# The MLP's second product of a diffusion trunk: all token tiles by one tile of weights in five banks, its weight sums on VectorE, and a fixed matmul order where the MLP begins

## The chip, the cores and the metric

The kernel runs on one core of a Trainium2 chip. The metric is the device time of one execution in microseconds (us), from three runs of each kernel. Five engines work side by side: TensorE (PE in the rows; its weight loads are PEld), VectorE (DVE), ScalarE (ACT), GpSimd (POOL) and SyncE (SP), which issues the transfers from and to HBM. Matmuls write into banks of PSUM; the other operands lie in SBUF.

## The reference, cut to what matters

One layer of a transformer over 128 context tokens and 512 latent tokens with shared weights, in float32. The change is in the last third, the MLP and the step into it:

```python
# _layer, D_MODEL = 1024, D_FF = 4096
y = _merge((o_a, o_b, o_c, o_d), u['gates'], P)          # ends with @ P['w_out']
x = x + g1 * _rmsnorm(y, P['norm_mix_post'])
h = _rmsnorm(x, P['norm_mlp_pre']) * (1 + sc2) + sh2
y = jnp.square(jax.nn.relu(h @ P['w_mlp_in'])) @ P['w_mlp_out']
x = x + g2 * _rmsnorm(y, P['norm_mlp_post'])
```

## The kernel before

The 640 tokens are five tiles of 128 (`NT = 5`; tiles 0 to 3 latent, tile 4 context). A float32 product is made from high and low parts: each operand is split into `hi` (rounded) and `lo` (the rest), and three matmuls, hi by hi, hi by lo and lo by hi, replace one. A weight tile is loaded raw (`wr`, 128x1024), copied to `wh` (by ACT, or by POOL in `copy_r`, line 139) and its rest `wl` is taken by DVE (`rest`, line 142). The tags `wr`, `wh` and `wl` have three buffers each in SBUF.

**The end of the mixing block.** For each token tile the second column half of `w_out` is multiplied (`tok_block`, 24 matmuls, lines 381 to 383), normed (`finish_half`, `finish`), normed again for the MLP (line 1293), and `to_h2` turns it: eight transposes on PE (`tp`, line 1243), eight scaled copies on ACT (`h2f`, line 1246), the high part on POOL, the low part on DVE. The result `h2T` is kept in two halves of 320 tokens (`HALF`), so that tile 2 lies in both halves and tile 4 is the last 128 columns of the second.

**The MLP** goes over eight quarters `qd` (`NQ = 8`) of 512 hidden features. Quarter 0 is made plainly: four blocks `m` by two halves of tokens, 24 matmuls of 128x320 each (`products`, lines 1319 to 1321). Each other quarter is two calls of `pair`: seven products of 12 matmuls (128x320), a scheme that saves one product in eight by sums of weights (`weight_sums`, lines 1347 to 1352) and sums of tokens (`token_sums`, `tsum`); its results are put together by adds (line 1371), squared after the relu (line 1310) and split again into `hid`. A product goes into one of five PSUM banks of the tag `pr`.

**The second product** of quarter `qd` is `out_of(qd)`: for each column half `j` two weight tiles (four blocks of 128 hidden features), and for each token tile 12 matmuls of 128x512 into one of two banks of the tag `mm`; then `done` adds the bank to the running sum `y2` on DVE (line 1402; a copy on ACT for quarter 0, line 1400). Only in the last quarter the half j = 0 goes otherwise: five banks, the first two blocks of weights over all five token tiles, then the other two. In the last quarter `done` also scales by the norm's gains on POOL (line 1260), norms (lines 1265 and 1269) and writes out.

The program's order is `pair(1,0)`, `out_of(0)`, `pair(1,1)`, `pair(2,0)`, `out_of(1)`, and so on, with `out_of(qd)` ahead of the second pair of the quarter after; a scheduler then orders the instructions of each engine by simulated time, except in stretches under `in_order`, which chains all instructions of an engine in the order in which they are written. "A period" below is what recurs: one `out_of` (120 matmuls of 128x512) and two pairs (168 of 128x320).

Of the kernel before, what the change touches and what calls it, by code (L numbers as in the profile page):

```python
# [17 lines left out]
D = 1024  # L18
# [46 lines left out]
def trunk(ctx, tc, I, O):  # L65
# [1214 lines left out]
    for tt in range(NT):  # L1280
        finish_half(banks[tt], x1(tt), tt, 0, G1, ssqs[:, 0, tt], V)
    w = [(w_hi[:, k], w_lo[:, k]) for k in range(4)] + wgroup(wo, 512, 512, k0=4, nk=4)
    for tt in range(NT):
        ps = tok_block(w, 512, yX, tt)
        finish_half(ps, x1(tt), tt, 1, G1, ssqs[:, 0, tt], V)
        x = mxa.tile([128, D], F32, tag="x", name="x", bufs=3)
# [50 lines left out]
    def weight_sums(c0):  # L1337

        r1, r2 = (wload(w1, 0, c0 + 128 * m, 128, 8) for m in range(2))
        sa = wp.tile([128, 1024], F32, tag="wr", name="ws")  # L1340
        p, q = slice(0, 512), slice(512, 1024)

        def split(x, nk):
            hi, lo = wsplit(x, 128, nk)
            return [[(hi[:, k], lo[:, k]) for k in range(i, i + 4)] for i in range(0, nk, 4)]
        a11, a12 = split(r1, 8)
        V.tensor_tensor(out=sa[:, q], in0=r2[:, p], in1=r2[:, q], op=ALU.add)  # L1347
        V.tensor_tensor(out=sa[:, p], in0=sa[:, q], in1=r1[:, p], op=ALU.subtract)
        g2, g1 = split(sa, 8)
        G.tensor_tensor(out=r2[:, p], in0=r1[:, p], in1=r2[:, p], op=ALU.subtract)  # L1350
        g3, a22 = split(r2, 8)
        G.tensor_tensor(out=r1[:, q], in0=r1[:, q], in1=sa[:, p], op=ALU.subtract)
        g4, = split(r1[:, q], 4)
        return a11, a12, a22, g1, g2, g3, g4

    def pair(c0, X, hid):
# [9 lines left out]
        def part(name):  # L1366
            return mxb.tile([128, HALF], F32, tag=name, name=name, bufs=1)

        def add(eng, p, q, out=None):
            out = relu2_tile() if out is None else out  # L1370
            eng.tensor_tensor(out=out, in0=p, in1=q, op=ALU.add)
# [40 lines left out]
    def out_of(qd):  # L1412

        for j in range(2):
            w = wgroup(w2, 512 * j, 512, k0=4 * qd, nk=4)
            if qd == NQ - 1 and j == 0:

                banks = [psl.tile([128, 512], F32, tag="pr", name="last", bufs=5) for _ in range(NT)]
                for k in (0, 2):
                    for tt in range(NT):  # L1420
                        tok_block(w[k:k + 2], 512, hid[qd][k:k + 2], tt, banks[tt], start=(k == 0), stop=(k == 2))
                        if k:
                            done(qd, tt, j, banks[tt])
                continue
            for tt in range(NT):
# [3 lines left out]
    hid[0] = [x for _ in range(2) for x in blocks_of(big(F32R, 2, 2, T, name="hid"))]
    for ms in ((0, 1, 2), (3,)):  # L1430
        ws = {m: wgroup(w1, 128 * m, 128) for m in ms}
        for th in range(2):
            for m in ms:
                ps, sq = mm_tile()[:, 0:HALF], relu2_tile()
                products(ps, ws[m], by_k(h2[0][th]) + by_k(h2[1][th]))
                S.activation(out=sq, in_=ps, func=AF.Relu)
                to_hid(sq, hid[0][m], HALF * th)
# [49 lines left out]
```

## Time and profile before

| | before |
|---|---|
| median of 3 runs | 1496.71 us |
| lowest and highest | 1494.04 and 1497.32 us |
| the profiled execution, its own time | 1497.44 us |
| its span, first to last instruction | 1495.7 us |
| mean granted TensorE clock | 0.989 |
| busy: PE, DVE, ACT, POOL | 94%, 61%, 35%, 32% of the span |

The span is 1.7 us shorter than the profiled execution's own time, and that execution is 0.7 us longer than the median. Times in the rows are counted from the span's start. The MLP begins at about 1019 us, where the transposes of tile 2 follow the last matmul of `w_out`, and its last matmul starts at 1484.57. A busy PE counts the modelled length of each matmul, which is longer than the distance from one start to the next; distances between starts tell its pace.

### The profile page before, as it was taken

The page shows a single profiled execution, that of the slowest core. Times are in us where ns is not written, and L with a number is a line of the kernel's source. Part 1 is how long each engine was busy: PE and PEld are TensorE (multiplying, and loading weights), DVE is VectorE, ACT ScalarE, POOL GpSimd, SP SyncE. Part 2 cuts the span into 40 slices and gives each one's busy share as a digit, 9 for nine tenths or more (in the row PEclk, how much of TensorE's full clock was granted, in tenths as well). Part 3 has the DMA queues.
Part 4 walks back from the last instruction along what each step waited for, and adds up shares of the span by engine and source line. Part 5 has one row for each costly group of instructions (what it writes and reads, how often), then busy time and mean ns, then how long its engine had stood idle before and what let it go on. Part 6 is the DMA issues. An engine that isn't in the chain of part 4 may idle for free.

```text
span 1495.7 us, 26614 instructions
## 1 busy us (share of the span) xinstructions
PE 1411.4 (94%) x10801; PEld 1279.3 (86%) x10801; DVE 909.8 (61%) x1587; ACT 519.7 (35%) x1189; POOL 481.6 (32%) x486
## 2 busy tenths in 40 slices
PE   6999999999999999999998998999999999899997
PEld 5898999999898998999996677988887888888885
DVE  4347757476643787433725566748755757857756
ACT  4334333333443235442125565226331221211212
POOL 2015326243322435222314334125322322223224
PEclk9999999999999999999999999999999999999998
DMA  9421222131112131113224601232213512312221
GB/s 331 127 85 58 72 58 59 44 75 43 45 46 57 43 75 37 41 35 78 78 66 162 205 15 43 99 88 68 85 57 113 155 43 85 99 43 85 86 82 72
DMA packets 138227, 121.17 MB, mean 81 GB/s; under 512 B 22297, under 2 KB 119413, under 8 KB 138105
## 3 DMA queue, kind: packets, MB, share of 16 engines
q1 hardware_dynamic: 138104, 119.47, 26.9%
q8 instruction: 85, 1.39, 0.4%
q14 instruction: 38, 0.30, 0.1%
HBM read 115.96 MB, written 3.49 MB: 80 GB/s over the span
## 4 chain that ended last, share of the span: by engine, by line
PE 68%; DVE 15%; POOL 5%; issue 5%; ACT 4%; DMA 3%; POOLq 0%; DVEq 0%; ACTq 0%
PE mm L365 8%; PE mm L366 8%; PE mm L367 8%; PE mm L381 5%; PE mm L382 5%; PE mm L383 5%; DVE wl L142 4%; PE tp L860 3%; PE pv L1013 3%; PE sc L383 3%; PE sc L381 2%; PE sc L382 2%; PE sc L953 2%; DVE relu L1310 2%; PE sc L954 2%
## 5 line engine op out<-in xcount | busy, mean ns | idle before, releaser
L142 DVE TENSOR_TENSOR wl<-wr,wh 128x1024 fp32r<-128x1024 f32 (+3 forms) x174 | 214.1, 1234 | 133.7 <-POOL wh L139 94.9
L139 POOL TENSOR_SCALAR wh<-wr 128x1024 fp32r<-128x1024 f32 (+2 forms) x108 | 123.5, 1147 | 341.5 <-PE mm L366 113.3
L365 PE MATMUL mm<-hTh,wh 128*128 128x320 f32 x704 | 220.4, 313 | 2.0 <-DVE qA L520 0.9
L367 PE MATMUL mm<-hTh,wl 128*128 128x320 f32 x704 | 219.1, 311 | 0.0
L366 PE MATMUL mm<-hTl,wh 128*128 128x320 f32 x704 | 218.1, 310 | 0.0
L813 POOL TENSOR_SCALAR P<-P,rden 128x640 f32<-128x640 f32 (+3 forms) x120 | 84.9, 717 | 183.5 <-DVE rden L825 87.3
L365 PEld LDWEIGHTS mm<-hTh,wh 128*128 128x128 f32 x704 | 132.2, 188 | 3.9 <-DVE qA L520 1.0
L367 PEld LDWEIGHTS mm<-hTh,wl 128*128 128x128 f32 x704 | 132.2, 188 | 0.9 <-issue 0.7
L366 PEld LDWEIGHTS mm<-hTl,wh 128*128 128x128 f32 x704 | 132.2, 188 | 0.5 <-issue 0.3
L382 PE MATMUL mm<-wl,hid 128*128 128x512 f32 x300 | 118.6, 395 | 4.8 <-DVE wl L142 4.8
L381 PE MATMUL mm<-wh,hid 128*128 128x512 f32 x300 | 117.2, 396 | 4.3 <-DVE y L1402 3.1
L383 PE MATMUL mm<-wh,hid 128*128 128x512 f32 x300 | 117.6, 392 | 0.0
L329 ACT ACTIVATE wh<-wr 128x1024 fp32r<-128x1024 f32 (+1 forms) x66 | 63.6, 965 | 90.9 <-PE mm L383 55.4
L1402 DVE TENSOR_TENSOR y<-mm,y 128x512 f32<-128x512 f32 x65 | 44.5, 687 | 68.0 <-PE mm L383 67.9
L381 PE MATMUL sc<-wh,hTh 128*128 128x256 f32 (+2 forms) x224 | 71.8, 321 | 5.4 <-DVE tx L939 2.4
L1321 PE MATMUL pr<-tsum,wl 128*128 128x320 f32 x224 | 69.0, 314 | 7.5 <-DVE wl L142 7.5
L860 PE MATMUL tp<-ident,P 128*128 128x128 f32 x456 | 72.5, 280 | 3.0 <-DVE modcol L242 1.1
L598 POOL TENSOR_TENSOR hk<-hk,hf 128x640 f32<-128x640 f32 x28 | 56.2, 2028 | 55.9 <-DVE hf L599 25.1
L1350 POOL TENSOR_TENSOR wr<-wr 128x512 f32<-128x512 f32 x14 | 31.2, 2228 | 132.3 <-DVE ws L1347 132.3
L381 PEld LDWEIGHTS mm<-wh,hid 128*128 128x128 f32 x300 | 56.5, 189 | 19.5 <-DVE y L1402 5.7
L382 PEld LDWEIGHTS mm<-wl,hid 128*128 128x128 f32 x300 | 56.7, 189 | 17.9 <-DVE wl L142 6.5
L383 PE MATMUL sc<-wh,hTl 128*128 128x256 f32 (+2 forms) x224 | 71.1, 317 | 0.2
(392 smaller groups left out, 3778.7 us busy)
## 6 DMA issues: line engine op xcount, KB each, us to landing
wr<-in_w_in SPq DMA_DIRECT2D x56, 512.0 KB, 3.8
wada<-in_w_ada SPq DMA_DIRECT2D x48, 512.0 KB, 4.9
wr<-in_w_mlp_in SPq DMA_DIRECT2D x32, 512.0 KB, 4.2
wr<-in_w_mlp_out SPq DMA_DIRECT2D x32, 512.0 KB, 3.7
wr<-in_w_in SPq DMA_DIRECT2D x64, 64.0 KB, 2.2
wr<-in_w_branch SPq DMA_DIRECT2D x8, 512.0 KB, 3.9
wr<-in_w_branch SPq DMA_DIRECT2D x16, 256.0 KB, 4.2
wr<-in_w_out SPq DMA_DIRECT2D x8, 512.0 KB, 3.6
```

Of the source, the lines that this page charges most:

```text
L139: G.tensor_scalar(out=out, in0=src, scalar1=1.0, scalar2=1.0, op0=ALU.mult, op1=ALU.mult)
L142: V.tensor_tensor(out=out, in0=src, in1=f(hi), op=ALU.subtract)
L329: S.activation(out=hi[:, 0:m], in_=raw[:, 0:m], func=AF.Copy)
L365: PE.matmul(out=ps[:, 0:tn], lhsT=wh, rhs=a, start=(k == 0), stop=False)
L366: PE.matmul(out=ps[:, 0:tn], lhsT=wh, rhs=b, start=False, stop=False)
L367: PE.matmul(out=ps[:, 0:tn], lhsT=wl, rhs=a, start=False, stop=(k == nk - 1))
L381: PE.matmul(out=ps[:, 0:n], lhsT=a, rhs=w[k][0], start=(start and k == 0), stop=False)
L382: PE.matmul(out=ps[:, 0:n], lhsT=a, rhs=w[k][1], start=False, stop=False)
L383: PE.matmul(out=ps[:, 0:n], lhsT=b, rhs=w[k][0], start=False, stop=(stop and k == nk - 1))
L813: G.tensor_scalar(out=Pt[:, i, 0:W], in0=Pt[:, i, 0:W], scalar1=rden[:, i:i + 1], scalar2=1.0, op0=ALU.mult, op1=ALU.mult)
L860: PE.transpose(out=tp[:, kk, i], in_=Pt[:, i, 128 * (kt + kk):128 * (kt + kk) + 128], identity=ident)
L1321: PE.matmul(out=ps, lhsT=w[k][1], rhs=x[k][0], start=False, stop=(stop and k == len(w) - 1))
```

## The change

Three things are changed. (1) `out_of` takes, for every quarter and both halves j, five `pr` banks; the first two blocks of weights (one `wr` tile) go over all five token tiles, then the other two, and `done` of a token tile comes after its second part. (2) Two of the weight sums of a pair and two of its adds are on DVE instead of POOL. (3) At the MLP's seam the PE order is written out under `in_order(PE)`: the norm's transposes of a token tile come two tiles later, three blocks of the first half of tokens come between those of tiles 2, 3 and 4, and block 0 of the second half is split into its first 192 and its last 128 columns, so that it has 48 matmuls instead of 24. The fourth block of quarter 0 follows after.

```diff
-    for tt in range(NT):
+    xs = {}
+    def second_half(tt):
         ps = tok_block(w, 512, yX, tt)
...
-        for kh in range(2):
-            to_h2(x, tt, kh)
+    def second_norm(tt):
+        for kh in range(2):
+            to_h2(xs[tt], tt, kh)
...
+    def block(w, m, th, parts=((0, HALF),)):
+        ps, sq = mm_tile()[:, 0:HALF], relu2_tile()
+        for a, b in parts:
+            products(ps[:, a:b], w, [(x[:, a:b], y[:, a:b]) for x, y in by_k(h2[0][th]) + by_k(h2[1][th])])
+        S.activation(out=sq, in_=ps, func=AF.Relu)
+        to_hid(sq, hid[0][m], HALF * th)
...
+    with in_order(PE):
+        for tt in range(NT):
+            second_half(tt)
+            if tt >= 2:
+                second_norm(tt - 2)
...
+        for m in range(3):
+            ws[m] = wgroup(w1, 128 * m, 128)
+            block(ws[m], m, 0)
+            if m:
+                second_norm(m + 2)
+        mn.close()
+        block(ws[0], 0, 1, ((0, 192), (192, HALF)))
+        for m in range(1, 3):
+            block(ws[m], m, 1)
...
         g2, g1 = split(sa, 8)
-        G.tensor_tensor(out=r2[:, p], in0=r1[:, p], in1=r2[:, p], op=ALU.subtract)
+        V.tensor_tensor(out=r2[:, p], in0=r1[:, p], in1=r2[:, p], op=ALU.subtract)
         g3, a22 = split(r2, 8)
-        G.tensor_tensor(out=r1[:, q], in0=r1[:, q], in1=sa[:, p], op=ALU.subtract)
+        V.tensor_tensor(out=r1[:, q], in0=r1[:, q], in1=sa[:, p], op=ALU.subtract)
...
-        u4 = add(G, u2, p5, part("u4"))
+        u4 = add(u2, p5, part("u4"))
...
-        to_hid(add(G, u3, p5), hid[1], HALF)
+        to_hid(add(u3, p5), hid[1], HALF)
...
             w = wgroup(w2, 512 * j, 512, k0=4 * qd, nk=4)
-            if qd == NQ - 1 and j == 0:
-                banks = [psl.tile([128, 512], F32, tag="pr", name="last", bufs=5) for _ in range(NT)]
...
-            for tt in range(NT):
-                done(qd, tt, j, tok_block(w, 512, hid[qd], tt))
+            banks = [psl.tile([128, 512], F32, tag="pr", name="out", bufs=5) for _ in range(NT)]
+            for k in (0, 2):
+                for tt in range(NT):
+                    tok_block(w[k:k + 2], 512, hid[qd][k:k + 2], tt, banks[tt], start=(k == 0), stop=(k == 2))
+                    if k:
+                        done(qd, tt, j, banks[tt])
```

**On PE, at the end of a period.** `mm` and `out` are banks of the second product (the number tells banks apart), `hid` its tokens, `pr` banks of the next pair's products. Before, from the second token tile of j = 1 on:

```order
L381 MATMUL mm_13827<-wh_13823,hid_13439 128x512
L382 MATMUL mm_13827<-wl_13824,hid_13439 128x512
L383 MATMUL mm_13827<-wh_13823,hid_13439 128x512
L1319 MATMUL pr_13925<-h2T_10873,wh_13903 128x320
L1320 MATMUL pr_13925<-h2T_10873,wh_13903 128x320
L1319 MATMUL pr_13939<-h2T_10875,wh_13903 128x320
L1320 MATMUL pr_13939<-h2T_10875,wh_13903 128x320
L381 MATMUL mm_13841<-wh_13817,hid_13119 128x512
L382 MATMUL mm_13841<-wl_13818,hid_13119 128x512
L383 MATMUL mm_13841<-wh_13817,hid_13119 128x512
```

The same place of the change, from the last part of the first pass into the second, and then the end of the half:

```order
L381 MATMUL out_13855<-wh_13841,hid_13143 128x512
L382 MATMUL out_13855<-wl_13842,hid_13143 128x512
L383 MATMUL out_13855<-wh_13841,hid_13143 128x512
L381 MATMUL out_13851<-wh_13847,hid_13463 128x512
L382 MATMUL out_13851<-wl_13848,hid_13463 128x512
L383 MATMUL out_13851<-wh_13847,hid_13463 128x512
```
```order
L382 MATMUL out_13855<-wl_13848,hid_13463 128x512
L383 MATMUL out_13855<-wh_13847,hid_13463 128x512
L1317 MATMUL pr_13949<-h2T_10873,wh_13927 128x320
L1318 MATMUL pr_13949<-h2T_10873,wh_13927 128x320
L1319 MATMUL pr_13949<-h2T_10873,wl_13928 128x320
```

The second tile of weights (`wh_13823` before, `wh_13847` now) is first read after all five tiles have gone through the first one, not within the first token tile; and no product of the next pair lies between the token tiles any more.

**On DVE, in the first pair of a period of the change** (the second pair's raw weights are `wr_13611` and `wr_13613`, its sums `ws_13615`; L1382 to L1387 are the weight sums, L1406 the adds):

```order
L1406 TENSOR_TENSOR u2_13536<-p1_13489,pr_13523 128x320
L1382 TENSOR_TENSOR ws_13615<-wr_13613 128x512
L142 TENSOR_TENSOR hid_13463<-relu2_13518,hid_13463 128x320
L1383 TENSOR_TENSOR ws_13615<-ws_13615,wr_13611 128x512
L1385 TENSOR_TENSOR wr_13613<-wr_13611,wr_13613 128x512
L142 TENSOR_TENSOR wl_13617<-wr_13611,wh_13616 128x1024
L1406 TENSOR_TENSOR u4_13552<-u2_13536,p5_13490 128x320
L1406 TENSOR_TENSOR u3_13567<-u2_13536,pr_13554 128x320
L1387 TENSOR_TENSOR wr_13611<-wr_13611,ws_13615 128x512
L1406 TENSOR_TENSOR relu2_13569<-u3_13567,p5_13490 128x320
L1406 TENSOR_TENSOR relu2_13587<-u4_13552,pr_13574 128x320
L142 TENSOR_TENSOR wl_13623<-ws_13615,wh_13622 128x1024
```

Rows L1385 and L1387, `u4` and the first `relu2` stood on POOL before, whose rows from one pair to the next now hold copies `wh<-wr` alone.

**On PE, at the seam**, before (the first line is the last matmul of `w_out`, `tp` are the transposes) and now, each from that line on:

```order
L383 MATMUL mm<-wh,yXl 128x512
L1243 MATMUL tp<-ident,x 128x128 x12
L1319 MATMUL mm<-h2T,wh 128x320 x2
L1243 MATMUL tp<-ident,x 128x128 x4
L1320 MATMUL mm<-h2T,wh 128x320
```
```order
L383 MATMUL mm<-wh,yXl 128x512
L1243 MATMUL tp<-ident,x 128x128 x8
L1317 MATMUL mm<-h2T,wh 128x320
L1318 MATMUL mm<-h2T,wh 128x320
L1319 MATMUL mm<-h2T,wl 128x320
```
```order
L1319 MATMUL mm<-h2T,wl 128x320
L1243 MATMUL tp<-ident,x 128x128 x8
L1317 MATMUL mm<-h2T,wh 128x192
L1318 MATMUL mm<-h2T,wh 128x192
L1319 MATMUL mm<-h2T,wl 128x192
```

Before, the transposes of tiles 2 and 3 stood together at the head of the MLP; now those of tile 3 come after the second block and those of tile 4 (the last rows) after the third, with the narrow matmuls behind them.

## Rows read from the trace of the kernel before

**Rows 1.** The page, its first section: busy time and share of the span of each engine.

```profile
PE 1411.4 (94%) x10801; PEld 1279.3 (86%) x10801; DVE 909.8 (61%) x1587; ACT 519.7 (35%) x1189; POOL 481.6 (32%) x486
```

**Rows 2.** The page of stretches: the stretch in us from the span's start, its length, busy time and count of PE, PEld, DVE, ACT, POOL, then the granted PE clock, the DMA share and GB/s. First a stretch of the `w_out` product that already runs five banks with the weights split in two passes, then the seam's head, then the MLP from `out_of(0)` to the last matmul, then the tail.

```profile
980.00:1006.70 26.70, 26.70 (x119) 22.08 (x118) 11.28 (x20) 7.00 (x18) 3.77 (x5) 1.00 0.27 75
1019.42:1025.98 6.56, 3.28 (x20) 2.70 (x18) 6.12 (x10) 4.89 (x16) 5.81 (x7) 0.84 0.28 80
1068.57:1484.96 416.39, 396.42 (x2142) 346.06 (x2140) 276.43 (x370) 94.52 (x161) 121.12 (x95) 0.99 0.27 83
1484.96:1495.70 10.74, 0.00 (x0) 0.00 (x0) 6.87 (x11) 0.92 (x4) 4.51 (x4) 0.65 0.39 146
```

**Rows 3.** The waits of PE from 1068.57 to 1484.9 us: what waited, for what, us in total, times, longest.

```profile
PE pr L1321 <- DVE wl L142: 8.1, 6, 2.1
PE mm L382 <- DVE wl L142: 4.8, 3, 1.8
PE mm L381 <- DVE y L1402: 3.1, 4, 0.8
PE ada L211 <- DMA wada<-in_w_ada: 2.2, 2, 1.4
PE mm L381 <- ACT y L1400: 1.2, 1, 1.2
PE mm L1209 <- DVE G L1212: 0.7, 1, 0.7
```

**Rows 4.** PE in order of time inside a pair: start, us, engine, line, operation; in brackets the idle time before it and what ended it.

```profile
1289.71 0.31 PE L1320 MATMUL pr<-tsum,wh 128*128 128x320 f32 x1
1291.44 0.41 PE L1321 MATMUL pr<-tsum,wl 128*128 128x320 f32 x1 [1.42 <-DVE wl L142]
1291.69 0.30 PE L1319 MATMUL pr<-tsum,wh 128*128 128x320 f32 x1
1291.83 0.31 PE L1320 MATMUL pr<-tsum,wh 128*128 128x320 f32 x1
```

**Rows 5.** PE in order of time at the head of a second product, the same columns.

```profile
1305.20 0.50 PE L382 MATMUL mm<-wl,hid 128*128 128x512 f32 x1 [1.82 <-DVE wl L142]
1305.54 0.39 PE L383 MATMUL mm<-wh,hid 128*128 128x512 f32 x1
1305.77 0.40 PE L381 MATMUL mm<-wh,hid 128*128 128x512 f32 x1
...
1308.54 0.50 PE L381 MATMUL mm<-wh,hid 128*128 128x512 f32 x1 [0.78 <-DVE y L1402]
```

**Rows 6.** The page of stretches again (columns as in rows 2): one whole period, two stretches of 3.4 us each after a wait, and one behind the first of them.

```profile
1251.74:1308.54 56.80, 52.79 (x288) 47.01 (x288) 39.33 (x53) 12.44 (x20) 15.62 (x12) 1.00 0.25 74
1235.55:1238.95 3.40, 3.40 (x15) 3.40 (x14) 3.40 (x7) 1.46 (x3) 0.00 (x0) 0.50 0.62 173
1239.00:1242.40 3.40, 3.40 (x25) 3.40 (x24) 3.26 (x6) 0.80 (x2) 2.13 (x2) 1.00 0.80 254
1419.90:1423.30 3.40, 3.40 (x10) 2.62 (x9) 3.25 (x6) 0.47 (x1) 0.00 (x0) 0.50 0.61 167
```

**Rows 7.** DVE, then POOL, in order of time around the weight sums of the pair of rows 4, and from the page the time of a load of `wr` from its issue to its landing.

```profile
1283.69 0.69 DVE L1347 TENSOR_TENSOR ws<-wr 128x512 f32<-128x512 f32 x1 [3.24 <-DMA wr<-in_w_mlp_in]
1284.30 1.22 DVE L142 TENSOR_TENSOR wl<-wr,wh 128x1024 fp32r<-128x1024 f32 x1
1285.44 1.78 DVE L1348 TENSOR_TENSOR ws<-ws,wr 128x512 f32<-128x512 f32 x1
...
1289.49 1.89 DVE L142 TENSOR_TENSOR wl<-ws,wh 128x1024 fp32r<-128x1024 f32 x1
```
```profile
1284.52 2.16 POOL L1350 TENSOR_TENSOR wr<-wr 128x512 f32<-128x512 f32 x1 [17.72 <-DVE ws L1347]
1286.64 1.33 POOL L1371 TENSOR_TENSOR u<-u,p 128x320 f32<-128x320 f32 x1
```
```profile
wr<-in_w_mlp_in SPq DMA_DIRECT2D x32, 512.0 KB, 4.2
```

**Rows 8.** PE at the seam in order of time: the head (tiles 2 and 3) and the transposes of tile 4 with the matmul that waited for them.

```profile
1019.42 1.03 PE L1243 MATMUL tp<-ident,x 128*128 128x128 f32 x8
1023.74 0.93 PE L1243 MATMUL tp<-ident,x 128*128 128x128 f32 x4 [3.28 <-DVE x L1293]
...
1033.14 1.03 PE L1243 MATMUL tp<-ident,x 128*128 128x128 f32 x8
...
1038.47 0.41 PE L1320 MATMUL mm<-h2T,wh 128*128 128x320 f32 x1 [0.33 <-DVE h2T L142]
```

**Rows 9.** The tail in order of time: DVE, then POOL. `y` is the running sum, L1260 its scaling by the gains, L1265 and L1269 the norm.

```profile
1487.06 0.68 DVE L1402 TENSOR_TENSOR y<-mm,y 128x512 f32<-128x512 f32 x1
1487.80 1.42 DVE L1269 SCALAR_TENSOR_TENSOR y<-y,rstd,x 128x512 f32<-128x512 f32 x2
1489.13 1.22 DVE L1265 TENSOR_TENSOR rstd<-ssqs 128x1 f32<-128x1 f32 x1
...
1491.21 1.42 DVE L1269 SCALAR_TENSOR_TENSOR y<-y,rstd,x 128x512 f32<-128x512 f32 x2 [0.66 <-POOL rstd L197]
```
```profile
1475.70 1.29 POOL L1260 TENSOR_TENSOR y<-y,G 128x512 f32<-128x512 f32 x1 [0.31 <-ACT junk L1259]
...
1485.23 1.70 POOL L1260 TENSOR_TENSOR y<-y,G 128x512 f32<-128x512 f32 x1 [0.86 <-ACT junk L1259]
```

More of the change, by code (lines that the diff above doesn't have):

```diff
@@ L1282, in trunk @@
     w = [(w_hi[:, k], w_lo[:, k]) for k in range(4)] + wgroup(wo, 512, 512, k0=4, nk=4)
-    for tt in range(NT):
+    xs = {}
+    def second_half(tt):
         ps = tok_block(w, 512, yX, tt)
         finish_half(ps, x1(tt), tt, 1, G1, ssqs[:, 0, tt], V)
-        x = mxa.tile([128, D], F32, tag="x", name="x", bufs=3)
+        x = xs[tt] = mxa.tile([128, D], F32, tag="x", name="x", bufs=3)
         dma(out=x, in_=x_rows(tt))
@@ L1321, in products @@
             PE.matmul(out=ps, lhsT=w[k][1], rhs=x[k][0], start=False, stop=(stop and k == len(w) - 1))
+    def block(w, m, th, parts=((0, HALF),)):
[4 more added lines that the diff above has]
+        to_hid(sq, hid[0][m], HALF * th)
+    w1, w2 = plain(I['w_mlp_in'][0]), plain(I['w_mlp_out'][0])
+    hid = {0: []}
+    with in_order(PE):
[3 more added lines that the diff above has]
+                second_norm(tt - 2)
+        for _ in range(2):
+            x = big(F32R, 2, 2, T, name="hid")
+            hid[0] += [(x[:, 0, m], x[:, 1, m]) for m in range(2)]
+        ws = {}
+        for m in range(3):
[7 more added lines that the diff above has]
+            block(ws[m], m, 1)
+    mxb = ctx.enter_context(tc.tile_pool(name="mxb", bufs=1))
+    y2 = rows_of("y2", mxb)
+    NQ = 8
+    w = wgroup(w1, 128 * 3, 128)
+    for th in range(2):
+        block(w, 3, th)
     def token_sums():
@@ L1367, in part, with add @@
             return mxb.tile([128, HALF], F32, tag=name, name=name, bufs=1)
-        def add(eng, p, q, out=None):
+        def add(p, q, out=None):
             out = relu2_tile() if out is None else out
-            eng.tensor_tensor(out=out, in0=p, in1=q, op=ALU.add)
+            V.tensor_tensor(out=out, in0=p, in1=q, op=ALU.add)
             return out
@@ L1375, in pair @@
         p2 = product(a12, b21)
-        to_hid(add(V, p1, p2), hid[0], 0)
-        u2 = add(V, p1, product(g2, t2), part("u2"))
+        to_hid(add(p1, p2), hid[0], 0)
+        u2 = add(p1, product(g2, t2), part("u2"))
         S.activation(out=p5, in_=product(g1, t1), func=AF.Copy)
-        u4 = add(G, u2, p5, part("u4"))
-        u3 = add(V, u2, product(g3, t3), part("u3"))
-        to_hid(add(G, u3, p5), hid[1], HALF)
-        to_hid(add(V, u4, product(g4, b22)), hid[0], HALF)
-        to_hid(add(V, u3, product(a22, t4)), hid[1], 0)
+        u4 = add(u2, p5, part("u4"))
+        u3 = add(u2, product(g3, t3), part("u3"))
+        to_hid(add(u3, p5), hid[1], HALF)
+        to_hid(add(u4, product(g4, b22)), hid[0], HALF)
+        to_hid(add(u3, product(a22, t4)), hid[1], 0)
     def blocks_of(tile):
         return [(tile[:, 0, m], tile[:, 1, m]) for m in range(2)]
-    hid = {}
     def pair_of(qd, p):
@@ L1415, in out_of @@
             w = wgroup(w2, 512 * j, 512, k0=4 * qd, nk=4)
-            if qd == NQ - 1 and j == 0:
-                banks = [psl.tile([128, 512], F32, tag="pr", name="last", bufs=5) for _ in range(NT)]
-                for k in (0, 2):
-                    for tt in range(NT):
[L1421 to L1425, printed above, removed]
-                done(qd, tt, j, tok_block(w, 512, hid[qd], tt))
[L1429 to L1437, printed above, removed]
+            banks = [psl.tile([128, 512], F32, tag="pr", name="out", bufs=5) for _ in range(NT)]
[4 more added lines that the diff above has]
+                        done(qd, tt, j, banks[tt])
     X = token_sums()
```

5 lines of the change are left out of this document (removed).

## The prediction

> **What bounds the kernel now.** I began with the page's busy shares: PE is busy 94% of the span, no other engine over 61% [rows 1]. The kernel is bound by PE, and what a change can win is PE's idle time or its slow time in the stretch that it touches. The page of stretches gives that for the MLP: from `out_of(0)` to the last matmul 416.39 us with PE busy 396.42, so 20.0 us idle [rows 2]. PE's waits in the same stretch say for what: 20.1 us in 17 waits, 12.9 of them for low parts of weights that DVE makes (`wl`), 4.3 for a bank that `done` must empty (on DVE, for quarter 0 on ACT), 2.2 for the loads of `wada`, 0.7 for `G` [rows 3]. The timelines show two places of a period: inside a pair PE stands 1.42 us for `wl` [rows 4]; at the head of a second product it stands 1.82 us for the `wl` of the second weight tile and soon after 0.78 us for a bank [rows 5]. The tail after the last matmul has no PE at all, 10.74 us [rows 2].
>
> Two things lie beside the idle time. A wait costs more than its idle time: in rows 4 the start before the wait and the one behind it are 1.73 apart, which is 1.42 and the usual 0.147 and 0.16 more, and the next start follows after 0.25 instead of 0.147, so about 0.26 in all. And after two of the waits the granted clock is 0.50 for a stretch of 3.4 us: 15 matmuls where the stretch behind it has 25, so 10 of 0.147 or 1.5 us are lost, and in the other 10 matmuls, which at 0.227 are 2.3 us of the 3.4, so 1.1 lost [rows 6].
>
> **Change 1 and 2: the MLP from `out_of(0)` on.** The matmuls are the same in number and shape. Their usual distance is 0.227 us for 128x512 (1305.54 to 1305.77 [rows 5]) and 0.147 for 128x320 (two of them in 0.29, 1291.69 being followed at 1291.83 [rows 4]). A period is then 120 x 0.227 + 168 x 0.147 = 51.9 us, and the one shown takes 56.80 [rows 6].
>
> - Bank waits. With five banks a bank has 4 x 6 matmuls, 5.4 us, between its last matmul and the next use by the next half; an add takes 0.68 [rows 9]. The 4.3 us go.
> - The second weight tile of a half was needed after 6 matmuls (1.4 us), now after 30 (6.8 us). By the order of DVE and the rows' durations the `wl` in question comes about 0.7 us after the half begins, so it has 6 us of cover. The 4.8 us go.
> - The sums of weights. While POOL runs beside DVE, both are slow: L1348 takes 1.78 beside L1350 on POOL, where the same 128x512 form takes 0.69 alone, and `wl` 1.89 where it takes 1.22 [rows 7]; the POOL operations take 2.16 and 1.33. Moved to DVE they are two of 0.69 and two of 128x320, about 0.45 each scaled by columns, so 2.3 us per pair, while DVE gets back 1.09 and 0.67 at the two rows shown. DVE's 39.3 us of a period [rows 6] thus stay near 40 of 52: it is no bound, but its queue counts.
> - The chain that is late today: the raw weights land at 1283.69, and the low part of their sum is ready at 1289.49 + 1.89 = 1291.38, 7.7 us later, where PE waits [rows 4, 7]. In the change I placed DVE's rows at these durations behind the end T of a second product on PE. The second pair's load cannot be issued until a raw buffer is free, at about T + 2.75; with 4.2 us for the transfer [rows 7] it lands at T + 7. `ws`, one `hid`, `ws`, L1385 and the first `wl` behind it give T + 10.3; PE needs that at T + 12.35 (84 matmuls later). The second `wl` comes at about T + 14.1, needed at T + 15.9. So both waits vanish, with 2 us to spare: this is the thinnest place. Lower bound of the gain: the 7.7 us as they are today put the second `wl` at T + 14.7, still just in time; upper: nothing waits.
> - Two waits for `wada` (2.2): their loads stand in the same buffers' turn and come earlier with it. The wait for `G` (0.7) stays.
>
> Sum: 20.1 - 0.7 = 19.4 idle, 16 x 0.26 = 4.2 for resuming, 2.6 for the clock that no longer falls: **26.2 us less**.
>
> What could speak against five banks in turn is the clock. The `w_out` product ahead of the seam already runs so, weights in two passes over five banks, and there PE is busy without a gap for 26.70 us with 119 matmuls at clock 1.00 [rows 2]; I charge nothing. The Trainium skill, "TensorE: Matmul & The Clock Gate", section "A second HAM failure mode: psum-queue depth-cycling", tells of a kernel whose cycling through PSUM banks let the clock swing between its levels; by that rule the gain would be eaten, by the row it stays. [...]
>
> **Change 3: the seam.** Today PE stands 3.28 us between the transposes [rows 8]; the stretch of 6.56 us has 3.28 busy and a clock of 0.84 [rows 2]. In the change the eight transposes of tile 2 are followed at once by the first block, which needs tile 2's `h2T`; that comes from the same copies at the same time, so I take this gap as it is (0, between -0.5 and +1). What is added: (a) eight transposes of tile 3 that lay half in that gap now stand in the stream: eight take (1.03 - 0.26 of the last one's tail) + 0.11 = 0.88 us [rows 8], so +0.9; (b) block 0's second half has 48 matmuls of 192 and 128 columns for 24 of 320. The nearest row for 128 columns is the transposes' 0.11; at that pace 48 x 0.11 = 5.28 against 24 x 0.147 = 3.53, so +1.75. Lower bound: scaled between the distances of 512 and 320 columns, 0.094 and 0.067, that is 3.86, +0.3; upper: 0.12 and 0.11, +2.0; (c) tile 4. Today its transposes start at 1033.14 and the matmul that needs its low part can start at 1038.47, 5.3 us later [rows 8]. Now 0.88 of transposes and 24 x 0.11 = 2.64 lie between, 3.5 us. A wait of up to 1.8; I take 1.2, since less else stands in the queues. From this goes 0.4 for the wait of today. **Seam: +3.4, between 0 and +5.5.**
>
> **The tail.** Today the five `done` of the last half are 12 x 0.227 = 2.72 us apart, but DVE's turn per token tile is longer, 3.41 us from one L1269 to the next (1487.80 and 1491.21): the add 0.68, L1269 twice 1.42, L1265 1.22, which is a 128x1 operation and stands because POOL's L1260 (1.70 then) runs, plus small ones [rows 9]. So the tail is already bound by DVE and POOL taking turns. In the change the five tiles finish 6 x 0.227 = 1.36 apart, the first 5.4 us before the last matmul instead of 10.9. The work behind them begins 5.5 us later, relative to the end Z of PE, and is done at DVE's and POOL's pace. Today L1269 ends at Z + 7.7 (1491.21 + 1.42 against 1484.96). Quickest: the first L1260 at Z - 4.2 and then five L1260 of 1.3 and five L1269 of 1.42 in turn, 13.6, so Z + 9.4, +1.7. Slowest: the add of the first tile at Z - 5.2, four turns of 3.4 and 5.6 of the last tile (1487.06 to 1492.63), Z + 14, +6.3. DVE's new order has the adds ahead and L1269 behind, between the two: **+4**.
>
> **Sum:** -26.2 + 3.4 + 4.0 = -18.8 us. On the profiled execution's 1497.4 that is 1478.6; the median was 0.7 lower, so **1478 us** (1.2% less).
>
> **Rivals.**
> - *The weight chain slips (forecast's sign, smaller).* The 2 us of margin hang on one load and on DVE's queue, in which adds that wait for PE's products stand ahead of the second `wl`. For: today's chain is late in just this place in most periods [rows 3, 4]. Against: POOL no longer holds it up. If it is late by 1 to 2 us in each of seven periods, 7 to 14 us come back: 1485 to 1492.
> - *Seam and tail cost nothing*: the gap of 3.28 closes and the tail overlaps: 1467 to 1471. *Or both come at their upper bounds* (5.5 + 6.3): 1483 to 1487.
> - *Other side: the next pair starts into a wait.* Today some matmuls of the next pair stand between the token tiles of the half j = 1 (the first order piece shows four), so PE has work while a `wl` is made; now all five banks are taken and there is none. A period wins 26.2 / 7 = 3.7 us, of which seam and tail take 7.4 / 7 = 1.1; so slower begins where a weight tile makes PE stand 2.4 us per period (2.7 with the 0.26 for resuming), that is, where it comes 2.4 + 2.0 = 4.4 us later than in my timeline. At 6 us of slip: 7 x 4.3 = 30 back, 1508. Against: DVE has 12 us of slack in a period [rows 6], and the load's 4.2 us would have to double.
> - *Other side: the clock swings with the banks*, as the Trainium skill's section named above has it. As a mechanism of this kernel: one fall per column half, at the 1.5 us of rows 6, is 16 x 1.5 = 24 us, 1502. The row at 980 us speaks against it.
> - *The change does not do what it says*: the scheduler's order leaves the waits where they are, only the seam and tail change: 1504 down to 1495.
>
> **How the numbers follow.** A measurement of this kernel tells about 0.2%, 3 us, from no change. Forecast (1471 to 1483) 0.60; chain slips 0.14; seam and tail free 0.10; both dear 0.07; next pair into a wait 0.05; clock 0.02; nothing done 0.02. Faster: the first four, 0.91; the last three give slower 0.06 and same 0.03. The range 1467 to 1489 holds the forecast, both seam cases and half of the slip, 0.84.
>
> **What would show it.** Right: no wait of PE for `wl` in pairs, none for `y`, distances of 0.227 and 0.147 throughout, a period of 52 us, no stretch at clock 0.50 behind `out_of(0)`; POOL's rows in a pair only copies; the seam about 3 us longer up to the token-sum products; L1269 ending 11 to 12 us after the last matmul. Wrong: a wait for `wl` that recurs in each period at the second pair's first or third product, or a clock below 1.00 in a second product.

## The result and the profile after

| | before | after |
|---|---|---|
| median | 1497.01 us (4 runs, 1494.04 to 1499.78) | 1480.97 us (4 runs, 1478.84 to 1484.16) |
| ratio | | 0.9895, 95% interval 0.9868 to 0.9922 |
| span of the profiled execution | 1495.7 us | 1478.4 us |

The change makes the kernel 16 us or 1.05% faster; the prediction was 1478 us.

To see where the time went, the span is cut at four matmuls that both programs have: the last matmul of `w_out`, the first of `out_of(0)`, the last of all, and the end (all by the start times in the timeline of PE).

| stretch | before | after | difference | predicted |
|---|---|---|---|---|
| ahead of the last `w_out` matmul | 1019.19 | 1021.20 | +2.0 | 0 |
| seam and quarter 0, to `out_of(0)` | 49.38 | 54.26 | +4.9 | +3.4 |
| MLP, to the start of the last matmul | 416.00 | 388.34 | -27.7 | -26.2 |
| tail | 11.09 | 14.61 | +3.5 | +4.0 |
| span | 1495.66 | 1478.41 | -17.3 | -18.8 |

The first line is no work of the change: up to the transposes of tile 0 both programs issue the same PE instructions, and the 2.0 us are already there (1008.75 against 1006.73). It is how two executions differ: in the run below that alters the tail alone, the same matmul of `w_out` starts at 1014.99, 6.2 us earlier than with the change.

The page's first section of the change, beside [rows 1]:

```profile
PE 1408.9 (95%) x10825; PEld 1282.2 (87%) x10825; DVE 908.0 (61%) x1643; ACT 521.6 (35%) x1189; POOL 396.2 (27%) x430
```

The waits of PE from 1015 to 1475 us, the stretch that holds seam, MLP and tail, beside [rows 3]:

```profile
PE mm L1317 <- POOL h2T L139: 4.1, 2, 3.6
PE mm L1318 <- DVE h2T L142: 1.6, 2, 0.8
```

Only the seam waits now. All six rows of [rows 3] are gone, the one for `G` too. The page of stretches (columns as in [rows 2]): the half-clock stretch behind the seam's head, the MLP from `out_of(0)` on, the tail, and 51.90 us inside the MLP, one period:

```profile
1025.47:1032.30 6.83, 5.40 (x19) 5.06 (x20) 4.84 (x11) 1.15 (x2) 3.38 (x6) 0.50 0.52 146
1075.46:1464.20 388.74, 388.73 (x2142) 344.53 (x2140) 269.59 (x413) 96.43 (x160) 47.04 (x40) 1.00 0.28 85
1464.20:1478.40 14.20, 0.00 (x0) 0.00 (x0) 10.94 (x19) 1.45 (x4) 6.63 (x7) 0.68 0.49 185
1222.00:1273.90 51.90, 51.90 (x289) 46.57 (x288) 37.59 (x60) 12.99 (x21) 5.45 (x4) 1.00 0.27 82
```

From 1075.46 to 1464.20 PE is busy 388.73 of 388.74 us at clock 1.00: the MLP has no gap left and no stretch at half clock.

The thinnest place of the prediction, the sums of the second pair's weights, with the end T of the second product first (PE, then DVE; T is 1265.47, where the first `pr` matmul starts):

```profile
1265.47 0.30 PE L1317 MATMUL pr<-h2T,wh 128*128 128x320 f32 x1
```
```profile
1272.15 0.69 DVE L1382 TENSOR_TENSOR ws<-wr 128x512 f32<-128x512 f32 x1 [0.72 <-DMA wr<-in_w_mlp_in]
...
1273.16 0.69 DVE L1383 TENSOR_TENSOR ws<-ws,wr 128x512 f32<-128x512 f32 x1
1273.76 0.68 DVE L1385 TENSOR_TENSOR wr<-wr 128x512 f32<-128x512 f32 x1
1274.37 1.22 DVE L142 TENSOR_TENSOR wl<-wr,wh 128x1024 fp32r<-128x1024 f32 x1
...
1278.10 1.22 DVE L142 TENSOR_TENSOR wl<-ws,wh 128x1024 fp32r<-128x1024 f32 x1
```

The load lands at T + 6.7 (predicted 7), the first `wl` is ready at T + 10.1 (10.3), the second at T + 13.9 (14.1); every operation is back at its time alone, 0.69 and 1.22 where [rows 7] have 1.78 and 1.89.

The seam in order of time, beside [rows 8]:

```profile
1021.43 1.03 PE L1243 MATMUL tp<-ident,x 128*128 128x128 f32 x8
1026.09 0.64 PE L1317 MATMUL mm<-h2T,wh 128*128 128x320 f32 x1 [3.62 <-POOL h2T L139]
1027.53 0.63 PE L1318 MATMUL mm<-h2T,wh 128*128 128x320 f32 x1 [0.81 <-DVE h2T L142]
...
1044.49 0.27 PE L1319 MATMUL mm<-h2T,wl 128*128 128x192 f32 x1
1045.27 0.33 PE L1317 MATMUL mm<-h2T,wh 128*128 128x128 f32 x1 [0.50 <-POOL h2T L139]
1046.39 0.33 PE L1318 MATMUL mm<-h2T,wh 128*128 128x128 f32 x1 [0.79 <-DVE h2T L142]
```

Two waits at the head, two at tile 4. And the tail, DVE and then POOL, beside [rows 9]:

```profile
1462.53 3.44 DVE L1269 SCALAR_TENSOR_TENSOR y<-y,rstd,x 128x512 f32<-128x512 f32 x2
...
1471.24 4.06 DVE L1269 SCALAR_TENSOR_TENSOR y<-y,rstd,x 128x512 f32<-128x512 f32 x6
```
```profile
1462.46 2.96 POOL L1260 TENSOR_TENSOR y<-y,G 128x512 f32<-128x512 f32 x2
```

L1269 twice takes 1.42 alone and 3.44 beside POOL's two L1260. The last L1269 ends at 1475.30, which is 11.1 us behind the end of PE (1464.20); the prediction said 11 to 12.

### The profile page after: what moved, and what is told of

It is laid out like the page before. It is cut to its first block, busy times and chain, and to the rows that moved or that the text cites. A ratio compares the mean times of both kernels' runs of the same rounds, so it can differ in the third digit from the quotient of the medians.

```text
span 1478.4 us, 26650 instructions
## 1 busy us (share of the span) xinstructions
PE 1408.9 (95%) x10825; PEld 1282.2 (87%) x10825; DVE 908.0 (61%) x1643; ACT 521.6 (35%) x1189; POOL 396.2 (27%) x430
## 4 chain that ended last, share of the span: by engine, by line
PE 83%; DVE 8%; POOL 3%; ACT 3%; issue 3%; DMA 1%; DVEq 0%; POOLq 0%; ACTq 0%
PE mm L365 8%; PE mm L367 8%; PE mm L366 8%; PE out L381 5%; PE out L383 5%; PE out L382 5%; PE pr L1317 4%; PE pr L1318 4%; PE pr L1319 4%; PE tp L860 3%; PE pv L1013 3%; PE sc L383 3%; PE sc L381 3%; PE sc L382 2%; PE sc L953 2%
## 5 line engine op out<-in xcount | busy, mean ns | idle before, releaser
L142 DVE TENSOR_TENSOR wl<-wr,wh 128x1024 fp32r<-128x1024 f32 (+3 forms) x174 | 209.4, 1207 | 134.9 <-POOL wh L139 81.4
L383 PE MATMUL out<-wh,hid 128*128 128x512 f32 x320 | 124.8, 390 | 0.0
L382 PE MATMUL out<-wl,hid 128*128 128x512 f32 x320 | 124.6, 389 | 0.0
L381 PE MATMUL out<-wh,hid 128*128 128x512 f32 x320 | 123.5, 391 | 0.0
L1435 DVE TENSOR_TENSOR y<-out,y 128x512 f32<-128x512 f32 x70 | 47.3, 687 | 52.1 <-PE out L383 52.1
L381 PEld LDWEIGHTS out<-wh,hid 128*128 128x128 f32 x320 | 60.0, 188 | 14.2 <-issue 2.1
L383 PEld LDWEIGHTS out<-wh,hid 128*128 128x128 f32 x320 | 60.0, 188 | 13.4 <-issue 0.8
L598 POOL TENSOR_TENSOR hk<-hk,hf 128x640 f32<-128x640 f32 x28 | 56.6, 2041 | 55.9 <-DVE hf L599 25.0
L382 PEld LDWEIGHTS out<-wl,hid 128*128 128x128 f32 x320 | 60.1, 188 | 12.2
L382 PE MATMUL sc<-wl,hTh 128*128 128x256 f32 (+2 forms) x224 | 70.5, 315 | 0.0
```

The lines of the kernel that those rows point to most:

```text
L142: V.tensor_tensor(out=out, in0=src, in1=f(hi), op=ALU.subtract)
L381: PE.matmul(out=ps[:, 0:n], lhsT=a, rhs=w[k][0], start=(start and k == 0), stop=False)
L382: PE.matmul(out=ps[:, 0:n], lhsT=a, rhs=w[k][1], start=False, stop=False)
L383: PE.matmul(out=ps[:, 0:n], lhsT=b, rhs=w[k][0], start=False, stop=(stop and k == nk - 1))
```

## The experiments

The question was which part of the change removes which wait, and what the seam and the tail cost. Each ratio is to the kernel before on the same chip.

**Change 1 alone.** `out_of` as in the change; sums on POOL and seam as before.

```diff
-            if qd == NQ - 1 and j == 0:
...
-            for tt in range(NT):
-                done(qd, tt, j, tok_block(w, 512, hid[qd], tt))
+            banks = [psl.tile([128, 512], F32, tag="pr", name="out", bufs=5) for _ in range(NT)]
+            for k in (0, 2):
+                for tt in range(NT):
+                    tok_block(w[k:k + 2], 512, hid[qd][k:k + 2], tt, banks[tt], start=(k == 0), stop=(k == 2))
+                    if k:
+                        done(qd, tt, j, banks[tt])
```

> Only change 1 on the kernel before: five banks and two passes in every second product; weight sums and two adds stay on POOL, the seam as before. Theory (each part of the change removes its own waits): the bank waits (4.3 us) and the waits at a second product's head for the second weight tile (4.8) go, with 0.26 each for resuming, about 12 us; the waits for wl inside pairs stay near 8 us; the tail is 3.5 longer: 1497 - 12 + 3.5 = 1488. Rival R (change 1 alone gives it all, because loads and splits move earlier): no wait for wl in pairs, about -27 + 3.5, 1473. Rival S (POOL's sums are the whole cause): waits for wl elsewhere take the place of the removed ones, 1497 to 1500.

Measured: 1474.18 us, ratio 0.9864 (0.9846 to 0.9882). My theory, that each part removes its own waits, fell here; rival R had the number. The page of stretches for the MLP, then the same place as above (PE at T, DVE, POOL):

```profile
1068.84:1457.57 388.73, 388.73 (x2142) 344.51 (x2140) 269.94 (x362) 95.58 (x160) 108.99 (x93) 1.00 0.28 86
```
```profile
1258.86 0.30 PE L1319 MATMUL pr<-h2T,wh 128*128 128x320 f32 x1
```
```profile
1265.67 0.69 DVE L1347 TENSOR_TENSOR ws<-wr 128x512 f32<-128x512 f32 x1 [0.85 <-DMA wr<-in_w_mlp_in]
...
1266.68 1.79 DVE L1348 TENSOR_TENSOR ws<-ws,wr 128x512 f32<-128x512 f32 x1
1268.39 1.90 DVE L142 TENSOR_TENSOR wl<-wr,wh 128x1024 fp32r<-128x1024 f32 x1
...
1272.01 1.90 DVE L142 TENSOR_TENSOR wl<-ws,wh 128x1024 fp32r<-128x1024 f32 x1
```
```profile
1266.49 1.43 POOL L1350 TENSOR_TENSOR wr<-wr 128x512 f32<-128x512 f32 x1 [17.21 <-DVE ws L1347]
```

DVE's operations are still slow beside POOL's (1.79 for 0.69 alone, 1.90 for 1.22), and yet PE is busy 388.73 of 388.73 us. The first `wl` is ready at T + 11.4 and the second at T + 15.1; PE needs them at T + 12.35 and T + 15.9. So the chain of [rows 7] is slow, but in time. Before, T of that pair is here:

```profile
1277.25 0.30 PE L1319 MATMUL pr<-tsum,wh 128*128 128x320 f32 x1
```

From it, the load of [rows 7] lands at T + 6.4 and the second `wl` is ready at T + 14.1, no later than with change 1 (T + 6.8 and T + 15.1). So what has moved is the need, not the chain, and R's reason, loads and splits that come earlier, is not what this trace shows. Before, 24 matmuls of the next pair were drawn ahead between the token tiles (the first order piece of the change's section shows four), 3.5 us of the pair's 12.35 that no longer lay between T and the second pair.

**Change 2 alone.** Sums and adds on DVE (the diff's `G` to `V` lines), all else as before.

> Only change 2 on the kernel before: two weight sums and two adds of each pair on DVE. Theory: the waits for wl inside pairs (8.1 us, 6 times 0.26, and the half-clock stretch behind one of them, 1.5) go, the bank waits (4.3) and the head waits stay or shrink little: about -11, 1486. Rival R: less than 3 us of change, since the late load and not POOL makes wl late: 1494 to 1497. Rival S: nearly all waits go, -25, 1472.

Measured: 1483.00 us, ratio 0.9927 (0.9906 to 0.9947). The waits of PE in the MLP:

```profile
PE mm L381 <- DVE y L1402: 4.3, 5, 1.2
...
PE mm L382 <- DVE wl L142: 1.9, 3, 0.9
...
```

The waits inside pairs are gone, the bank waits stay, as the theory had it; the head waits fall from 4.8 to 1.9 as well, which it did not say. Some 24 matmuls are still drawn ahead in each period here. The chain behind one second product, from the landing of the load to the `wl` of the sum:

```profile
1271.90 0.69 DVE L1347 TENSOR_TENSOR ws<-wr 128x512 f32<-128x512 f32 x1 [2.61 <-DMA wr<-in_w_mlp_in]
...
1276.26 1.21 DVE L142 TENSOR_TENSOR wl<-ws,wh 128x1024 fp32r<-128x1024 f32 x1
```

It takes 5.6 us, where [rows 7] take 7.7. So a faster chain and a later need each remove the pairs' waits, and their gains do not add.

**Five banks in j = 1 only**, the half j = 0 in two banks, sums on POOL:

```diff
-            if qd == NQ - 1 and j == 0:
+            if j == 1:
```

> The kernel before with five banks and two passes in the column half j = 1 of every second product, the half j = 0 as before in two banks; POOL keeps its sums. With all five banks taken no matmul of the next pair is drawn ahead into the half j = 1 (before, 24 of 168 are). Theory D (the matmuls drawn ahead are what makes PE wait in the pairs: they bring the second pair's first product 24 x 0.147 = 3.5 us nearer, while its load is still bound to a buffer that is freed at the end of the second product): the waits for wl inside pairs go (8.1 idle, about 11 with resuming and clock), the head of j = 0 and its banks keep most of theirs (about 6 to 9), the tail costs 3.5: 1488 to 1491. Rival P (POOL's sums make wl late): the waits inside pairs stay, 1497 or more.

Measured: 1474.23 us, ratio 0.9856 (0.9841 to 0.9870): the pair waits are gone as theory D said, and the rest too, which it did not say. The MLP in the page of stretches, then DVE and PE at the head of a second product that begins at 1233.26:

```profile
1069.97:1459.40 389.43, 389.34 (x2142) 343.80 (x2140) 271.16 (x363) 95.15 (x160) 114.64 (x92) 1.00 0.28 86
```
```profile
1235.75 1.21 DVE L142 TENSOR_TENSOR wl<-wr,wh 128x1024 fp32r<-128x1024 f32 x1
```
```profile
1236.46 1.07 PE L381 MATMUL last<-wh,hid 128*128 128x512 f32 x4
1237.37 0.39 PE L382 MATMUL mm<-wl,hid 128*128 128x512 f32 x1
```

The second weight tile's `wl` is ready 3.7 us after the head, and PE first needs it 4.1 us after: the scheduler has put the first weight tile's matmuls of both token tiles that the two banks hold, and four matmuls of the half j = 1 (`last`, into the free banks), ahead of it.

**Five banks in j = 0 only**, j = 1 per token tile in two banks; 21 to 23 matmuls of the next pair are drawn ahead still.

```diff
-            if qd == NQ - 1 and j == 0:
+            if j == 0:
```

> The kernel before with five banks in the half j = 0 only, j = 1 per token tile in two banks; 22 or 23 matmuls of the next pair are still drawn ahead. Theory D: the waits for wl inside pairs stay near 8 us, the waits at the head and for banks go (about 9 idle, 12 in all), the tail is as before: 1485 to 1488. Rival (it is the head's waits that push the pairs late): all go, 1471.

Measured: 1476.94 us, ratio 0.9870 (0.9853 to 0.9887). The head's and the banks' waits are gone, and of [rows 3] this stays, with the wait for `G`:

```profile
PE pr L1321 <- DVE wl L142: 5.9, 6, 2.1
```

As theory D has it: six pair waits with matmuls drawn ahead, none without. The total is 8 us under the expectation. In the trace the MLP takes 399.2 us, 16.8 less than before, where about 12 were expected: the waits for `wada` go too (2.2 before), those in the pairs are 2.2 shorter, and one stretch of 3.4 us is at half clock (from 1391.32) where there were two. The other 3 us do not show in this trace, whose execution is the slowest of its four.

**Nothing but the order.** The kernel before, with PE's order of each second product and the pair behind it as written, so that nothing is drawn ahead:

```diff
-        out_of(qd)
-        if qd + 1 < NQ:
-            pair_of(qd + 1, 1)
+        with in_order(PE):
+            out_of(qd)
+            if qd + 1 < NQ:
+                pair_of(qd + 1, 1)
```

> The kernel before, its second products per token tile in two banks and its sums on POOL as they were; the one edit is that the PE order of out_of(qd) and the pair behind it is fixed as written, so that no matmul of the pair is drawn ahead. Theory D: the waits for wl inside pairs go (8.1 idle, 11 to 13 with resuming and clock), at most the bank waits stay (up to 4.3 idle, 5.5): 1479 to 1485. If the bank waits too came from the pairs' lateness: 1472. Rival Q (five banks are needed, since two banks let the adds run late): 1492 or more.

Measured: 1498.33 us, ratio 1.0017 (1.0005 to 1.0029), rival Q's number. The waits of PE in the MLP, then a head, PE and DVE:

```profile
PE mm L382 <- DVE wl L142: 9.6, 5, 2.2
PE ada L211 <- DMA wada<-in_w_ada: 5.9, 2, 3.0
...
PE mm L381 <- DVE y L1402: 1.4, 4, 0.4
```
```profile
1244.49 0.39 PE L381 MATMUL mm<-wh,hid 128*128 128x512 f32 x1
...
1248.90 0.50 PE L382 MATMUL mm<-wl,hid 128*128 128x512 f32 x1 [2.22 <-DVE wl L142]
```
```profile
1247.64 1.21 DVE L142 TENSOR_TENSOR wl<-wr,wh 128x1024 fp32r<-128x1024 f32 x1
```

Not one wait for `wl` inside a pair is left, so theory D holds for those. But they come back at the head: the second tile's `wl` is ready 4.4 us after the head, and per token tile it is needed after 6 matmuls. The fixed order also holds the `wada` matmuls in place (5.9), and 17 us of the MLP are at half clock, where it was 7 before. Rival Q's reason, late adds, is the least of these waits (1.4). A later need in one place is paid at the next unless that one gets cover too, and this is what five banks and two passes do at once.

**Change 3 alone**: the seam's order; the MLP behind it as before.

> Only change 3: the PE order at the seam, the rest as before. Theory: the seam, from the last matmul of w_out to the first matmul of out_of(0), takes 4.9 us longer as in the trace of the change (54.3 for 49.4), and the MLP behind it keeps its 20 us of waits: 1502. Rival: the seam's order starts the loads and weight splits of the MLP earlier and takes part of its waits away: 1490 to 1497.

Measured: 1497.45 us, ratio 1.0015 (1.0002 to 1.0028). The seam takes 55.1 us in its trace (49.4 before), but the MLP 410.5 (416.0), with these waits:

```profile
PE pr L1319 <- DVE wl L142: 6.4, 5, 1.8
...
PE mm L382 <- DVE wl L142: 3.8, 4, 1.1
PE mm L381 <- DVE y L1435: 3.3, 5, 0.8
```

The rival is half right: in this trace the MLP's waits add up to 16.0 us instead of 20.1, and it has one half-clock stretch instead of two. Over all runs the interval leaves 0.3 to 4.2 us for the whole kernel, less than the 5.7 by which the seam is longer in the trace, so a part is gained back as a rule. Why the seam's order should shorten these waits was not tested.

**Changes 1 and 2 without the seam.**

> Changes 1 and 2 without the seam (its order as the scheduler had it). Theory: the MLP gains its 27.7 us, the tail costs 3.5, the seam stays at 49.4: 1497 - 24 = 1473, and 5 to 8 us below the whole change. Rival: the seam is a part of the gain (it lets the MLP start with its buffers free), some waits are back: 1478 or more.

Measured: 1472.47 us, ratio 0.9852 (0.9834 to 0.9871). In its trace the seam takes 49.4 us, the MLP 388.3, the tail 14.6: the theory's numbers. It is only 1.7 us under change 1 alone, though the five runs of each, on one chip, do not overlap (1471.99 to 1473.68 against 1473.91 to 1475.28). The MLP takes 388.3 us and the tail 14.6 in both traces, so change 2 adds nothing there once change 1 is in; 0.8 of the difference lies in the seam (50.2 us with change 1 alone). The seam's order costs its 4.9 us without return.

**The seam: no split**, the rest as changed.

```diff
-        block(ws[0], 0, 1, ((0, 192), (192, HALF)))
+        block(ws[0], 0, 1)
```

> The whole change with block 0's second half in one piece of 320 columns (24 matmuls) at the same place. Theory: it saves 1.8 us of narrow matmuls and exposes all of tile 4's way, 5.3 us from its transposes less their 0.9, so 4.4 of wait instead of 1.7: 1 us slower than the change, up to 3 if the clock falls behind the wait. Rival (the split is pure cost): 1.8 faster.

Measured: 1480.83 us, ratio 0.9901 (0.9884 to 0.9918), the same as the change. In the trace the seam takes 56.6 instead of 54.3: the wait for tile 4 is 3.2 and 0.7 us instead of 0.5 and 0.8, and behind it the clock is at its half for 3.4 us, as it is not in the trace of the change. The run with the tail's scaling on DVE (below) has the split and such a half-clock stretch at tile 4 too, and its seam takes 55.3. So by the traces the split is worth its narrow matmuls, by 1.3 us with the clock alike; the medians do not tell the two apart.

**The seam: tiles 3 and 4 one block earlier, and no split.**

```diff
-            if m:
-                second_norm(m + 2)
+            if m < 2:
+                second_norm(m + 3)
...
-        block(ws[0], 0, 1, ((0, 192), (192, HALF)))
+        block(ws[0], 0, 1)
```

> The whole change with another order at the seam: the transposes of tiles 3 and 4 each one block earlier, and block 0's second half not split. Theory (the split costs 1.8 us and tile 4's low part 1.7 us because only 24 narrow matmuls lie ahead of it): with a whole block of 3.5 us ahead the wait falls to about 0.9 and the split's 1.8 goes: 2.5 below the change, 1478. Rival (the seam's cost lies in its head, tile 2 and the clock behind it): within 1 us of the change.

Measured: 1474.97 us, ratio 0.9865 (0.9844 to 0.9886); the seam takes 50.7 us, 3.6 less. PE's waits from 1015 to 1475:

```profile
PE mm L1317 <- POOL h2T L139: 3.6, 1, 3.6
PE mm L1318 <- DVE h2T L142: 1.4, 2, 0.8
```

The head's 3.6 and 0.8 are as they were; at tile 4 only 0.6 is left. The theory holds for tile 4 and the split (0.9 and 1.8). The remaining 0.9 lies in the half-clock stretch behind the head, which lasts 3.4 us in this trace and 6.8 in that of the change. The page of stretches for it, here and then with change 2 alone:

```profile
1025.67:1029.08 3.41, 3.41 (x15) 3.41 (x14) 2.39 (x6) 0.88 (x1) 1.05 (x2) 0.50 0.51 145
```
```profile
1020.48:1027.31 6.83, 5.54 (x22) 5.36 (x23) 6.83 (x12) 3.71 (x12) 5.93 (x8) 0.50 0.54 154
```

With change 2 alone the seam has the order and the waits of before (3.3 and 0.3), but 6.8 us at half clock, where the kernel before has 3.4, and it takes 50.3 us instead of 49.4. So 3.4 us more at half clock cost 0.9 us, with either order.

**The tail: last half per token tile**, the rest as changed.

```diff
+            if qd == NQ - 1 and j == 1:
+                for tt in range(NT):
+                    done(qd, tt, j, tok_block(w, 512, hid[qd], tt))
+                continue
```

> The whole change, but the last half (quarter 7, j = 1) goes per token tile in two banks as before. Theory: the tail from the last matmul's start to the end falls from 14.6 to 11.1 us, nothing else moves: 3.5 below the change, 1477. Rival: one of the last half's first weight tile or bank waits comes back (up to 2.6): 1479 to 1480.

Measured: 1477.09 us, ratio 0.9863 (0.9839 to 0.9888). In its trace the tail is 11.06 us (14.61), the MLP 388.34 as with the change, without a wait: the theory to the tenth.

**The tail: the last half's scaling by the gains on DVE.**

```diff
-            finish_half(ys, y2(tt), tt, j, G2, ssqs[:, 1, tt], G)
+            finish_half(ys, y2(tt), tt, j, G2, ssqs[:, 1, tt], G if j == 0 else V)
```

> The whole change, but the scaling by the gains in the last half is on DVE instead of POOL. Theory (DVE and POOL take turns in the tail): five operations of 0.68 more on DVE, none of its operations stands beside POOL's, L1269 back at 0.7 each: DVE's work behind the first add is 5 x (0.6 + 0.6 + 1.34 + 0.3) = 14 us from Z - 5.2, so it ends near Z + 9 instead of Z + 11.5: 2 to 3 below the change, 1478. Rival (the tail is bound by DVE's own work): the added 3 us stand on the path, 1484.

Measured: 1477.99 us, ratio 0.9878 (0.9861 to 0.9895); the tail is 12.34 us in the trace, 2.3 less, although DVE does five operations more. `L1269` twice takes about 1.4 us for every tile here. That POOL's scaling holds DVE up in the tail is shown by this.

**The best of these together**: changes 1 and 2, the seam as before, the last half per token tile, its scaling on DVE.

> Changes 1 and 2, the seam as before, the last half per token tile in two banks, and its scaling by the gains on DVE. Theory: seam 49.4, MLP 388.3, and the tail below the 11.1 us of before, since DVE's turn per token tile falls from 3.4 to about 2.9 and no longer accumulates behind PE's 2.72: about 8.5: 1472.5 - 6 = 1466. Rival: the tail stays at 11, 1469.

Measured: 1469.26 us, ratio 0.9820 (0.9800 to 0.9839), faster than both kernels. The seam takes 49.1 us, the MLP 388.3, the tail 10.6, not 8.5: the rival was right on the tail. Three of DVE's turns, the last ones:

```profile
1456.68 1.42 DVE L1269 SCALAR_TENSOR_TENSOR y<-y,rstd,x 128x512 f32<-128x512 f32 x2 [0.67 <-POOL rstd L197]
...
1460.09 1.42 DVE L1269 SCALAR_TENSOR_TENSOR y<-y,rstd,x 128x512 f32<-128x512 f32 x2 [0.66 <-POOL rstd L197]
...
1463.03 1.42 DVE L1269 SCALAR_TENSOR_TENSOR y<-y,rstd,x 128x512 f32<-128x512 f32 x2 [0.66 <-POOL rstd L197]
```

POOL's scaling no longer stands in the way, but L1269 waits 0.66 or 0.67 us for POOL's power (L197) each time, where in [rows 9] it was L1265 that stood beside POOL's L1260. From 1456.68 to 1460.09 the turn is 3.41 us as before; only the last one, with no add of a next tile in it, is 2.94.

## Why the prediction was right, point by point

- **The total** came this close with some luck: the MLP gained 1.5 us more than predicted and the seam cost 1.5 more, which cancel, and the tail cost 0.5 less. These three make -19.3; the 2.0 us ahead of the change make it -17.3.
- **The MLP** (-26.2, measured -27.7). The sum of waits, resuming and clock held; the wait for `G`, which I left in, went too. The timeline by T, worked out from the order and the rows' durations, came within 0.3 us at each of its steps.
- **Its cause** was told too broadly. I priced the two changes as one sum, with POOL's interference as what makes the chain late. My own lower bound said that the 7.7 us of [rows 7] would still be in time; change 1 alone shows it (T + 15.1 against 15.9), so change 2 was not needed for these waits. What I did not see is that the matmuls drawn ahead into the half j = 1 were the other half of the cause. In the rivals I counted them as cover that would be lost. They were the reverse: five banks in the half j = 1 forbid them, and the pair waits go.
- **Bank and head waits** went as said. For the head, the two passes give the cover of 30 matmuls (6.8 us); fixing the order alone, with 6 matmuls of cover, leaves 9.6 us there.
- **The clock.** The MLP runs at clock 1.00 with five banks in turn through all of its 388.74 us. The Trainium skill, "TensorE: Matmul & The Clock Gate", section "A second HAM failure mode: psum-queue depth-cycling", tells of a kernel whose clock swung with such cycling, and gives as the reason that PE idled for short times between its groups of matmuls. Neither the row at 980 us nor this MLP has such idle time (388.73 us busy of 388.74), so trace and section do not contradict each other. The prediction read the rule without its condition; that the gain would be eaten by it did not follow.
- **The seam** (+3.4, measured +4.9; predicted terms in brackets). Split: 48 matmuls at 0.111 are 5.3 for 3.5, +1.8 (1.75). Tile 4: the two waits cost 1.7 (1.2; up to 1.8 was the bound). What went were today's wait and its resuming, 0.8 (0.4). The mis-sized term is the head, with the eight transposes: 0 and 0.9, together 0.9, against 2.2 measured as the excess over the usual distances up to the end of the slow stretch (7.4 against 5.2). The gap itself is as long as before, but [rows 2] had eight transposes and two matmuls in it, and now PE stands 3.62 and 0.81 us with one matmul between. Behind it the clock is at its half for 6.8 us instead of 3.4 (0.50 in the row above), with 0.267 us from one matmul to the next. By the two rows under the last seam run, 0.9 of the 2.2 is this longer stretch, which the head's order alone does not decide; the other 1.3 are near the predicted 0.9.
- **The tail** (+4.0, measured +3.5): the turns of DVE and POOL, as worked out.

## What to carry to other kernels

A scheduler that fills a gap with the next stage's matmuls takes cover from the loads that the next stage is bound to: where PE waits in a steady loop, look at what was drawn ahead of the wait and not only at the slow chain behind it. Giving each pass over the tokens as many banks as there are token tiles gives a late second weight tile 30 matmuls of cover instead of 6; but in the last pass, with an output chain behind each token tile, the old order is worth 3.5 us. And of an edit of several parts, each is worth its own run: one part gave nearly all of the gain here, one at most 1.7 us on top, one cost 5 us.

## What the runs showed of the hardware that was not expected

- A matmul of 192 columns is as long as one of 128: in the seam of the change twelve of either take 1.34 us, 0.11 each, where 320 columns take 0.147. Cutting 320 into 192 and 128 takes 0.22, half as much again.

```profile
1042.26 0.27 PE L1317 MATMUL mm<-h2T,wh 128*128 128x192 f32 x1
...
1043.60 0.27 PE L1317 MATMUL mm<-h2T,wh 128*128 128x192 f32 x1
...
1046.55 0.28 PE L1319 MATMUL mm<-h2T,wl 128*128 128x128 f32 x1
...
1047.89 0.28 PE L1319 MATMUL mm<-h2T,wl 128*128 128x128 f32 x1
```

- Behind the seam's head the clock was at its half for 3.4 us or for 6.8 us, at like waits of PE (3.3 with the old order, 3.6 and 0.8 with the new). With the old order seven traces have 3.4 and one has 6.8; with the new order five have 6.8 and one has 3.4. The order shifts the odds, as far as fourteen traces can tell, but what decides in one execution is not shown.
- The last `w_out` matmul ahead of the seam started between 1014.99 and 1021.20 us in the fourteen profiled executions shown here (before, after and twelve runs), whose PE program is the same up to there but for the place of a few transposes, so that profiled spans differ by up to 6 us without any cause in the change. Stretches cut at common matmuls are comparable; spans of single executions are not.
